# Four edits to a fused decoder-layer kernel: decay-row layout, sample-state engines, weight-sum order, sample-key order

## The chip, the cores and the metric

The kernel runs as one launch on one core of a Trainium2 chip. Five engines work side by side, each on its own instruction list in order: TensorE (PE), VectorE (DVE), ScalarE (ACT), GpSimd (POOL) and SyncE (SP), which here only issues DMAs. The metric is the device time of one execution in microseconds (us); lower is better.

## The reference

One layer of a hybrid decoder is computed for a prompt of 1024 tokens and for 8 single sample tokens, which share all weights. In short:

```python
xn = rmsnorm(x)                                  # prompt and sample tokens
sc_b, sc_c, sc_x, z, xbc, dt, q, gates = split(xn @ w_in)
y_a = (sc_b * conv3(sc_c * sc_x)) @ w_sc_out     # gated convolution
xs, bm, cm = split(silu(conv4(xbc) + bias))      # state-space branch, 32 heads x 64, state 128, 4 groups
# prompt: chunks of 128 tokens; acum = cumsum(dt * a) in the chunk
#   y = (cb * exp(acum_i - acum_j)) @ xdt + exp(acum) * (c @ state);  state = decay * state + b.T @ (...)
# sample: s = s * exp(dt * a) + (dt * x) outer b;   y = s . c         (state_ssm in, s_ssm out)
y_b = group_rmsnorm((y + d * xs) * silu(z)) @ w_ssm_out
y_c = softmax(q . mem_k / 16) @ mem_v @ w_attn_o # prompt: keys from mem; sample: cache_mem_k, cache_mem_v
x = x + (g_a * y_a + g_b * y_b + g_c * y_c) @ w_merge_o
x = x + (silu(xn2 @ w_gate) * (xn2 @ w_up)) @ w_down
y = rmsnorm(x)                                   # outputs: y, memory keys and values, all new states
```

## The kernel before

Matrices are held transposed: 128 features on the partitions, the 1032 tokens (1024 + 8) along the row. Every float32 product is made as three products of rounded halves (high with high, high with low, low with high), so each weight block of 128 x 1024 is loaded by SP, rounded to a high half by ACT (`st_split` and `weights`, lines 220 and 146) and its low half is made by DVE. The pool of weight halves has three slots, and `in_turn` (line 110) fixes the order in which they are written.

The stages follow one another. First come the norm and the dt values (`dt_rows`, line 551, writes the cumulated decays to the scratch tensor `ac_d` and their exponentials to `ea_d`). Then the z and xBC columns are projected two blocks at a time by `strassen` (line 274), which needs seven products instead of eight: the first weight block as it stands (A), then sums of blocks that DVE forms in `sa` (S) and `sb` (T, "third weight sums", `st_sums2`, line 266), then D. While the z pairs run, the memory keys and values are projected too (`kv_block`, line 1100), one half block at each `tick()`. `tick` (line 168) takes the next piece of side work from the list `pend`.

Then comes the state-space stage: for each of 4 groups, 8 chunks of pieces `p1`, `p2`, `p3` (line 906 on) run beside ordinary projections (`gemm`, line 180), three pieces to one projection. `load` (736) fetches a chunk's decay rows into `r`, copied to all 128 partitions, `prep` (743) makes the exponentials on ACT, `first`, `second` and `third` use PE and DVE, and one sample token's state goes through `s_load`, `s_step` and `s_read` (lines 870 to 893). In `s_step` DVE makes an outer product, and POOL multiplies the state by its decay and adds. `s_read` stores the state and reduces it on DVE.

The attention stage runs in the same way beside the output projections (`out_part`, line 1424). Prompt heads go through `a_scores`, and three pieces later `a_probs`. The sample's keys (`s_scores`, line 1250) are multiplied by the query on DVE; query and keys share the two buffers of the tag `kc`. After it `s_out` (1295) loads the sample's values. The feed-forward part uses `strassen` again (line 1632 on), and a down projection ends the layer.

The Tile framework orders the instructions of each engine before the run, by the readiness that its own planned times give and by their place in the program; `tc.issue_after(ins)` adds the rule that what is issued in the block on the engine of `ins` comes after it. On the chip each engine, and SP's list of DMAs, then keeps to that order, however long a wait takes.

## Time and profile before

| what | value |
|---|---|
| time, three runs | 2593.17, 2596.79, 2601.07 us (median 2596.79) |
| the profiled execution: time / span of the instructions | 2593.12 / 2591.4 us |
| TensorE (PE) busy | 2520.2 us, 97% |
| VectorE (DVE) busy | 1463.4 us, 56% |
| ScalarE (ACT) busy | 937.1 us, 36% |
| GpSimd (POOL) busy | 184.6 us, 7% |
| mean granted TensorE clock | 0.989 |

"Busy" adds up the time in which an engine runs at least one instruction. In the lists of waits each row names the waiting engine, its output and line, what it waited for, the sum in us, the count and the longest. Rows of the timeline start with start and duration in us; square brackets hold the idle time of the engine before the row and what ended it. "SPq" is SP issuing a DMA. Groups of instructions are shown by line with their count, busy time, mean duration in ns, and the idle time before them.

### The profile page before, as it was taken

The numbers are of one execution on the slowest core, as the hardware profiler recorded it, in microseconds if no ns is written. First come the engines' busy times: TensorE is split into PE (matmuls) and PEld (weight loads), VectorE is DVE, ScalarE is ACT, GpSimd is POOL, SyncE is SP. The second block draws the span as 40 slices with busy tenths as digits, with TensorE's granted clock in tenths as the row PEclk, the third lists the DMA queues.
The fourth block names the chain that finished last, engine by engine and source line by source line (L and its number), as shares of the span: only waits on it lengthen the run. The fifth ranks groups of instructions, "written<-read, shape, count | busy, mean of one in ns | idle before, by whom it ended". The sixth has DMA issues, their size and how long they took to land.

```text
span 2591.4 us, 42766 instructions
## 1 busy us (share of the span) xinstructions
PE 2520.2 (97%) x18037; PEld 2453.2 (95%) x18037; DVE 1463.4 (56%) x2049; ACT 937.1 (36%) x1436; POOL 184.6 (7%) x203
## 2 busy tenths in 40 slices
PE   7999999999999999999999999999999999999998
PEld 6899999989998999999999998999999999999998
DVE  5744586866667555555566633444685445453316
ACT  6643454553332334254352322222443333341202
POOL 0000000013213213123000000000000000000000
PEclk9999999999999999999999999999999999999999
DMA  5244333376646656666387757854442222265211
GB/s 191 94 139 155 118 112 107 123 193 154 163 150 135 173 173 169 182 183 160 115 300 240 271 177 252 291 199 135 136 155 85 74 88 71 77 218 159 66 41 66
DMA packets 394654, 394.59 MB, mean 152 GB/s; under 512 B 15782, under 2 KB 339990, under 8 KB 394455
## 3 DMA queue, kind: packets, MB, share of 16 engines
q1 hardware_dynamic: 375310, 338.90, 43.9%
q10 hardware_dynamic: 19153, 52.96, 5.3%
q8 instruction: 142, 2.33, 0.4%
q14 instruction: 49, 0.40, 0.0%
HBM read 283.57 MB, written 108.45 MB: 151 GB/s over the span
## 4 chain that ended last, share of the span: by engine, by line
PE 68%; DMA 5%; DVE 4%; ACT 1%; issue 1%; POOL 0%; SPq 0%; DVEq 0%; ACTq 0%; POOLq 0%
PE po L192 11%; PE ps_g L192 9%; PE pd L192 8%; PE ps_scc L192 4%; PE pm L1539 4%; PE ps_q L192 4%; PE ps_scx L192 3%; PE ps_scb L192 3%; DMA kc<-in_cache_mem_k_dram 2%; PE py L801 1%; PE pss L819 1%; PE po L793 1%; DMA r<-ac_d 1%; PE u20m L236 1%; PE g20m L236 1%
## 5 line engine op out<-in xcount | busy, mean ns | idle before, releaser
L1681 DVE TENSOR_TENSOR x<-pd,x 128x1032 f32<-128x1032 f32 x24 | 29.6, 1231 | 130.1 <-PE pd L192 130.1
L746 ACT ACTIVATE r<-r,acum 128x128 f32<-128x128 f32 x256 | 78.9, 391 | 36.2 <-DMA r<-ac_d 35.0
L1428 DVE TENSOR_TENSOR gt<-po,gt 128x1032 f32<-128x1032 f32 x24 | 29.5, 1229 | 74.7 <-PE po L192 68.0
L780 POOL TENSOR_TENSOR xdd<-xdt,decst 128x512 f32<-128x512 f32 x32 | 46.6, 1455 | 266.2 <-DVE xdt L776 266.2
L602 DVE SCALAR_TENSOR_TENSOR ax<-u,prm,ax 128x1024 f32<-128x1024 f32 x44 | 56.4, 1281 | 0.2
L886 POOL TENSOR_TENSOR st<-st,xb 128x512 f32<-128x512 f32 x32 | 44.8, 1401 | 36.2 <-DVE xb L880 34.0
L773 ACT COPY bT<-bp 128x128 f32<-128x128 f32 x32 | 8.4, 263 | 105.4 <-DVE cbm L771 105.4
L774 DVE TENSOR_TENSOR r<-r,cbm 128x1024 f32<-128x1024 f32 x32 | 39.1, 1221 | 9.6 <-ACT r L747 8.9
L810 DVE SCALAR_TENSOR_TENSOR x<-x,dpar,yt 128x128 f32<-128x128 f32 x128 | 37.4, 352 | 10.1 <-ACT yt L808 9.2
L832 POOL TENSOR_TENSOR s<-s,cdec 128x512 f32<-128x512 f32 x28 | 39.1, 1397 | 44.9 <-DVE s L825 36.8
L825 DVE TENSOR_TENSOR s<-pss,s 128x512 f32<-128x512 f32 x28 | 19.2, 687 | 36.7 <-PE pss L819 36.7
L819 PE MATMUL pss<-xdd,bT 128*128 128x512 f32 x64 | 33.8, 610 | 5.9 <-ACT bT L773 5.8
L883 POOL TENSOR_TENSOR st<-st,es 128x512 f32<-128x512 f32 x32 | 36.4, 1138 | 19.2 <-DMA st<-in_state_ssm_dram 15.6
L801 PE MATMUL py<-r,xdt 128*64 128x128 f32 x512 | 35.0, 279 | 2.5 <-issue 2.5
L771 DVE TENSOR_TENSOR cbm<-bp,tri 128x128 f32<-128x128 f32 x32 | 9.2, 289 | 46.8 <-PE bp L766 46.8
L747 ACT ACTIVATE r<-r 128x1024 f32<-128x1024 f32 x32 | 33.9, 1059 | 0.7
L797 DVE TENSOR_TENSOR yt<-po,ea 128x512 f32<-128x512 f32 x28 | 19.2, 686 | 25.9 <-PE po L793 25.9
L801 PEld LDWEIGHTS py<-r,xdt 128*64 128x64 f32 x512 | 27.3, 136 | 6.8 <-issue 3.4
L1267 ACT ACTIVATE pr<-psa,mx 128x256 f32<-128x256 f32 x32 | 14.9, 471 | 49.2 <-DVE mx L1265 49.1
L1468 DVE TENSOR_TENSOR gt<-po,gt 128x1032 f32<-128x1032 f32 x8 | 9.9, 1232 | 38.6 <-PE po L192 38.6
L1546 DVE TENSOR_TENSOR x<-pm,xT 128x516 f32<-128x516 f32 x16 | 11.1, 696 | 36.3 <-PE pm L1539 36.2
L1257 DVE TENSOR_TENSOR kc<-kc,qb 128x1024 f32<-128x1024 f32 x16 | 19.6, 1222 | 21.3 <-DMA kc<-in_cache_mem_k_dram 21.3
(7967 smaller groups left out, 8665.5 us busy)
## 6 DMA issues: line engine op xcount, KB each, us to landing
gt<-gt_d SPq DMA_DIRECT2D x32, 516.0 KB
r<-ac_d SPq DMA_DIRECT2D x32, 512.0 KB
gt_d<-g ACTq DMA_DIRECT2D x24, 516.0 KB
mg_d<-gt SPq DMA_DIRECT2D x24, 516.0 KB
mg<-mg_d SPq DMA_DIRECT2D x24, 516.0 KB
xs_d<-ax ACTq DMA_DIRECT2D x22, 516.0 KB
hr<-h_d SPq DMA_DIRECT2D x22, 516.0 KB
zs_d<-z ACTq DMA_DIRECT2D x16, 516.0 KB
```

The source lines that it names most:

```text
L192: PE.matmul(ps[:, n, :CW], wt[:, ks], x[:, n * CW : (n + 1) * CW], start=(k == 0 and i == 0), stop=(k == nk - 1 and i == 2),)
L236: PE.matmul(ps[:, n, :HC], wt[:, ks], x[:, n * HC : (n + 1) * HC], start=(start and kt == 0 and i == 0), stop=(kt == 3 and i == 2), skip_g ...
L602: V.scalar_tensor_tensor(acc[:, :T], u[:, j : j + T], w[j], acc[:, :T], op0=ALU.mult, op1=ALU.add)
L746: S.activation(r[:, h, :], r[:, h, :], AF.Relu, scale=-1.0, bias=acum[:, c, h0 + h : h0 + h + 1])
L774: V.tensor_tensor(r, r, bc(cbm.unsqueeze(1), [P, HPG, P]), op=ALU.mult)
L780: G.tensor_tensor(b3(xdd, HPG), b3(xdt, HPG), bc(decst[:, c, hs].unsqueeze(2), [P, HPG, 64]), op=ALU.mult)
L801: PE.matmul(py[hp : hp + 64, (h // 2) * P : (h // 2 + 1) * P], xdt[:, h * 64 : (h + 1) * 64], r[:, h, :], start=True, stop=True,)
L810: V.scalar_tensor_tensor(xg[t][:, cs], xg[t][:, cs], dpar[:, g * 4 + t : g * 4 + t + 1], yt[:, t, :], op0=ALU.mult, op1=ALU.add,)
L819: PE.matmul(pss, bT, xdd, start=True, stop=True)
L832: ins = G.tensor_tensor(b3(s_new, HPG), b3(state["s"], HPG), bc(cdec[:, c, hs].unsqueeze(2), [P, HPG, 64]), op=ALU.mult,)
L886: G.tensor_tensor(st, st, xb, op=ALU.add)
L1539: PE.matmul(ps[:, n, :HC], wt[:, ks], x[:, half * HT + n * HC : half * HT + (n + 1) * HC], start=(k == 0 and i == 0), stop=(k == KD - 1 an ...
```

## The change

The decay rows are stored so that the rows of one group and chunk lie together: `load` and `load_ea` then read one contiguous run for each partition instead of eight or four, and so does the read of `bc_d`; in return `dt_rows` writes with 20 DMAs instead of 2. The sample state is multiplied by its decay in four ACT instructions and updated by four DVE instructions, one per quarter; POOL no longer takes part, and the store of the state is issued after the load of a later chunk's decay rows. In `strassen` the sums `sb` are formed right after the S sums, and their split stands ahead of the `tick()`. In the attention stage the query has a buffer of its own, the keys are asked for two pieces ahead of their use, the sample work is spread over four pieces per token, `a_probs` stands ahead of `a_scores`, the `issue_after` rules of `both` are gone, the tag `pr` has three buffers instead of four, and the values are asked for ahead of `s_out`.

```diff
--- before.py
+++ after.py
@@ -263,13 +263,16 @@
         V.tensor_add(sa[:, 512:], sa[:, :512], raw1[:, :512])
         return raw1, raw2, sa, st_split(sa, f"{nm}S")
 
-    def st_sums2(raw1, raw2, sa, nm, sums):
+    def st_adds2(raw1, raw2, sa, nm, sums):
         sb = sums(f"{nm}sb")
         V.tensor_add(sb[:, :512], raw1[:, :512], raw2[:, :512])
         V.scalar_tensor_tensor(
             sb[:, 512:], sa[:, 512:], -1.0, raw1[:, 512:], op0=ALU.mult, op1=ALU.subtract
         )
-        return st_split(sb, f"{nm}T")
+        return sb
+
+    def st_sums2(*args):
+        return st_split(st_adds2(*args), f"{args[3]}T")
 
     def strassen(src1, src2, forms, nm, sums, outs, early=None, after_t3=None, ready=None):
 
@@ -299,6 +302,8 @@
             V.tensor_add(sa[:, :512], raw2[:, :512], raw2[:, 512:])
             V.tensor_add(sa[:, 512:], sa[:, :512], raw1[:, :512])
             wS = st_split(sa, f"{nm}S")
+        if ready is None:
+            sb = st_adds2(raw1, raw2, sa, nm, sums)
         prod(pb, wS, 0, "T1", True)
         S.copy(h3(o22), hv(pb))
         prod(pa, wS, 512, "nT2", early is not None)
@@ -310,9 +315,9 @@
             S.copy(o21, o12)
             V.tensor_sub(o22, o22, o12)
             V.tensor_tensor(h3(o12), hv(pa), h3(o12), op=ALU.add)
+        if ready is None:
+            wT = st_split(sb, f"{nm}T")
         tick()
-        if ready is None:
-            wT = st_sums2(raw1, raw2, sa, nm, sums)
         prod(pa, wT, 0, "T3", False)
         if after_t3 is not None:
             after_t3()
@@ -347,9 +352,9 @@
     q_d = dram("q_d", [8, P, TT])
     k_d = dram("k_d", [2, P, D])
     v_d = dram("v_d", [2, P, D])
-    ac_d = dram("ac_d", [HEADS, T])
-    ea_d = dram("ea_d", [HEADS, T])
-    bc_d = dram("bc_d", [GROUPS, 2, NS, P])
+    ac_d = dram("ac_d", [GROUPS, NCK, HPG, P])
+    ea_d = dram("ea_d", [GROUPS, NCK, 2, HPG // 2, P])
+    bc_d = dram("bc_d", [GROUPS, NS, 2, P])
     qs_d = dram("qs_d", [NS, D])
     os_d = dram("os_d", [NS, D])
 
@@ -557,8 +562,12 @@
             c = slice(half * 512, (half + 1) * 512)
             V.tensor_copy(act_[:, c], ps[:HEADS, :])
             S.activation(eat_[:, c], ps[:HEADS, :], AF.Exp)
-        SY.dma_start(ac_d, act_)
-        SY.dma_start(ea_d, eat_)
+        for g in range(GROUPS):
+            hs = slice(g * HPG, (g + 1) * HPG)
+            SY.dma_start(ac_d[g].rearrange("c h p -> h c p"), act_[hs].rearrange("h (c p) -> h c p", p=P))
+            ev_ = eat_[hs].rearrange("h (c p) -> h c p", p=P)
+            for t in range(HPG // 2):
+                SY.dma_start(ea_d[g, :, :, t].rearrange("c w p -> w c p"), ev_[2 * t : 2 * t + 2])
 
     def dt_sample():
 
@@ -725,7 +734,7 @@
         PE.transpose(ps[:NS, P : 2 * P], bcg[1][:, T:TT], ident)
         t = ev_tile(f"bcr{g}", (NS, 2, P))
         S.copy(t, b3(ps[:NS, : 2 * P], 2))
-        SY.dma_start(bc_d[g].rearrange("k b n -> b k n"), t)
+        SY.dma_start(bc_d[g], t)
 
     def ssd_pieces(g, xg, bcg):
         hs = slice(g * HPG, (g + 1) * HPG)
@@ -735,10 +744,9 @@
 
         def load(c):
             nm = f"{g}_{c}"
-            cs = slice(c * P, (c + 1) * P)
             r = sp_tile([P, HPG, P], "r", "r" + nm, 3)
-            SY.dma_start(r, ac_d[hs, cs].unsqueeze(0).to_broadcast([P, HPG, P]))
             live[c] = r
+            return SY.dma_start(r, ac_d[g, c].unsqueeze(0).to_broadcast([P, HPG, P])).ins
 
         def prep(c):
             r = live[c]
@@ -749,11 +757,9 @@
         def load_ea(c):
             ea = None
             if c > 0:
-                cs = slice(c * P, (c + 1) * P)
                 ea = sp_tile([P, 4, P], "ea", f"ea{g}_{c}")
-                eav = ea_d[hs, cs].rearrange("(t two) i -> two t i", two=2)
                 for k in range(2):
-                    SY.dma_start(ea[k * 64 : (k + 1) * 64], eav[k].unsqueeze(0).to_broadcast([64, 4, P]))
+                    SY.dma_start(ea[k * 64 : (k + 1) * 64], ea_d[g, c, k].unsqueeze(0).to_broadcast([64, 4, P]))
             return ea
 
         def first(c):
@@ -871,19 +877,17 @@
             st = sp_tile([P, 4, P], "st", f"st{g}_{b}", 3)
             SY.dma_start(st, s_rows(a["state_ssm"], b))
             bcb = sp_tile([P, 2, P], "bcb", f"bcb{g}_{b}")
-            SY.dma_start(bcb, bc_d[g, :, b, :].unsqueeze(0).to_broadcast([P, 2, P]))
+            SY.dma_start(bcb, bc_d[g, b].unsqueeze(0).to_broadcast([P, 2, P]))
             samp[b] = (st, bcb)
 
         def s_step(b):
             st, bcb = samp[b]
-            xb = sp_tile([P, 4, P], "xb", f"xb{g}_{b}", 1)
-            V.tensor_tensor(
-                xb, bc(bcb[:, 0:1, :], [P, 4, P]), bc(hold["xd"][:, :, b : b + 1], [P, 4, P]), op=ALU.mult
-            )
-            G.tensor_tensor(
-                st, st, bc(es[:, g * 4 : g * 4 + 4, b : b + 1], [P, 4, P]), op=ALU.mult
-            )
-            G.tensor_tensor(st, st, xb, op=ALU.add)
+            for t in range(4):
+                S.activation(st[:, t], st[:, t], AF.Copy, scale=es[:, g * 4 + t, b : b + 1])
+            for t in range(4):
+                V.scalar_tensor_tensor(
+                    st[:, t], bcb[:, 0], hold["xd"][:, t, b : b + 1], st[:, t], op0=ALU.mult, op1=ALU.add
+                )
 
         def s_read(b):
             st, bcb = samp.pop(b)
@@ -907,10 +911,11 @@
                 if c < NCK:
                     first(c)
                 if c + 2 < NCK:
-                    load(c + 2)
+                    state["load"] = load(c + 2)
                 if c > 1:
                     with tc.issue_after(state["xdt"] if c < NCK else state["sum"]):
-                        s_read(c - 2)
+                        with tc.issue_after(state["load"]):
+                            s_read(c - 2)
 
             def p2(c=c):
                 if c > 0:
@@ -1246,20 +1251,24 @@
                 V.tensor_sub(kTl[:, half * 4 : half * 4 + 4, m * P : (m + 1) * P], b3(ps, 4), kh.bitcast(F32))
 
         qbs = {}
+        kcs = {}
+
+        def s_query(b):
+            qbs[b] = at.tile([P, D], F32, tag="qb", bufs=1, name=f"qb{b}")
+            SY.dma_start(qbs[b], qs_d[b : b + 1, :].to_broadcast([P, D]))
+
+        def s_keys(b, m):
+            kcs[b, m] = at.tile([P, D], F32, tag="kc", name=f"kc{b}{m}")
+            SY.dma_start(kcs[b, m], a["cache_mem_k"][0, b, m * P : (m + 1) * P].rearrange("m h d -> m (h d)"))
 
         def s_scores(b, m):
-            if m == 0:
-                qbs[b] = at.tile([P, D], F32, tag="kc", name=f"qb{b}")
-                SY.dma_start(qbs[b], qs_d[b : b + 1, :].to_broadcast([P, D]))
-            qb = qbs[b]
-            kc = at.tile([P, D], F32, tag="kc", name=f"kc{b}{m}")
-            SY.dma_start(kc, a["cache_mem_k"][0, b, m * P : (m + 1) * P].rearrange("m h d -> m (h d)"))
-            V.tensor_mul(kc, kc, qb)
+            kc = kcs.pop((b, m))
+            V.tensor_mul(kc, kc, qbs[b])
             V.tensor_reduce(sc_s[:, m, b, :], b3(kc, AH), axis=AX.X, op=ALU.add)
 
         def softmax(pr, src, n, npart, name):
-            mx = at.tile([P, 2], F32, tag="mx", name="mx" + name)
-            sm = at.tile([P, 2], F32, tag="smx", name="sm" + name)
+            mxs = at.tile([P, 4], F32, tag="mx", name="mx" + name)
+            mx, sm = mxs[:, :2], mxs[:, 2:]
             sv = b3(src, n)
             V.tensor_reduce(mx[:npart, :n], sv, axis=AX.X, op=ALU.max)
             V.tensor_scalar(mx[:npart, :n], mx[:npart, :n], -1.0 / 16.0, None, op0=ALU.mult)
@@ -1281,7 +1290,7 @@
                 PE.transpose(
                     ps[:32, m * P : (m + 1) * P], sc_s[:, m].rearrange("p b h -> p (b h)"), ident
                 )
-            pr = at.tile([P, 2, MEM], F32, tag="pr", bufs=4, name="prs")[:32, :1]
+            pr = at.tile([P, 2, MEM], F32, tag="pr", bufs=3, name="prs")[:32, :1]
             softmax(pr, ps[:32, :MEM], 1, 32, "s")
             s_hold["pr"] = pr
 
@@ -1292,21 +1301,24 @@
                 PE.transpose(ps[:, m * 32 : (m + 1) * 32], pr[:, 0, m * P : (m + 1) * P], ident[:32, :32])
             V.tensor_copy(pTs.rearrange("p m c -> p (m c)"), ps[:, :64])
 
+        def s_values(b):
+            for m in range(2):
+                kcs[b, m] = at.tile([P, D], F32, tag="kc", name=f"vc{b}{m}")
+                SY.dma_start(kcs[b, m], a["cache_mem_v"][0, b, m * P : (m + 1) * P].rearrange("m h d -> m (h d)"))
+
         def s_out(b):
             ps = sm_ps(f"pso{b}")
-            vcs = []
-            for m in range(2):
-                vc = at.tile([P, D], F32, tag="kc", name=f"vc{b}{m}")
-                SY.dma_start(vc, a["cache_mem_v"][0, b, m * P : (m + 1) * P].rearrange("m h d -> m (h d)"))
-                vcs.append(vc)
+            vcs = [kcs.pop((b, m)) for m in range(2)]
             for m in range(2):
                 for h in range(AH):
                     PE.matmul(
                         ps[32 * h : 32 * h + 32, :256], pTs[:, m, :], vcs[m][:, h * 256 : (h + 1) * 256],
                         start=(m == 0), stop=(m == 1),
                     )
-            t = at.tile([P, 256], F32, tag="so", bufs=1, name=f"so{b}")
+            t = at.tile([P, 2, MEM], F32, tag="pr", bufs=3, name=f"so{b}")[:, 0]
             S.copy(t, ps[:, :256])
+            if b + 1 < NS:
+                s_values(b + 1)
             for h in range(AH):
                 row = 32 * h + b * AH + h
                 SY.dma_start(os_d[b : b + 1, h * 256 : (h + 1) * 256], t[row : row + 1, :])
@@ -1343,7 +1355,7 @@
                     PE.matmul(po, qh[:, ls], kh, start=(dk == 0), stop=False)
                     PE.matmul(po, qh[:, ls], kl, start=False, stop=False)
                     PE.matmul(po, ql[:, ls], kh, start=False, stop=(dk == 1))
-            pr = at.tile([P, 2, MEM], F32, tag="pr", bufs=4, name="pr" + nm)
+            pr = at.tile([P, 2, MEM], F32, tag="pr", bufs=3, name="pr" + nm)
             heads[h][2][l2] = pr
             return softmax(pr, ps, 2, P, nm)
 
@@ -1378,35 +1390,28 @@
                 S.copy(ot[:, c], ps)
             S.dma_start(at_d[2 * h + dk, :, :T], ot[:, :T])
 
-        def both(*fs):
-
-            def run():
-                ins = fs[0][0](*fs[0][1:]) if fs else None
-                for f, *args in fs[1:]:
-                    if ins is None:
-                        f(*args)
-                    else:
-                        with tc.issue_after(ins.ins):
-                            f(*args)
-
-            return run
-
-        pieces = [both((kv_in, 0)), both((kv_in, 1), (a_load, 0)), None, None]
-        side = deque([(s_scores, b, m) for b in range(NS) for m in range(2)])
-
-        def aside():
-            return (side.popleft(),) if side else ()
-
+        pieces = [[(kv_in, 0)], [(kv_in, 1), (a_load, 0)], [], []]
         for h in range(AH):
             for l2 in range(LAG + 4):
-                fs = [(a_scores, h, l2)] if l2 < 4 else []
                 late = [(a_probs, h, l2 - LAG)] if l2 >= LAG else []
-                pieces.append(both(*fs, *aside(), *late) if fs else both(*late, *aside()))
+                pieces.append(late + ([(a_scores, h, l2)] if l2 < 4 else []))
             if h + 1 < AH:
-                pieces.append(both((a_load, h + 1)))
-            pieces.append(both((a_out, h, 0)))
-            pieces.append(both((a_out, h, 1)))
-        pieces += [s_softmax, None, s_probs, None]
+                pieces.append([(a_load, h + 1)])
+            pieces.append([(a_out, h, 0)])
+            pieces.append([(a_out, h, 1)])
+        for b in range(NS):
+            at_ = 4 + 4 * b
+            for i, fs in enumerate(
+                ([(s_query, b), (s_keys, b, 0)], [(s_keys, b, 1)], [(s_scores, b, 0)], [(s_scores, b, 1)])
+            ):
+                pieces[at_ + i].extend(fs)
+
+        def run(fs):
+            for f, *args in fs:
+                f(*args)
+
+        pieces = [lambda fs=fs: run(fs) for fs in pieces]
+        pieces += [s_softmax, lambda: s_values(0), s_probs, None]
         for b in range(NS):
             pieces += [lambda b=b: s_out(b), None]
         pend.extend(pieces)
```

## The prediction

> **What bounds the kernel.** The first look goes to the page: how busy is each engine over the whole span?
>
> ```profile
> span 2591.4 us, 42766 instructions
> PE 2520.2 (97%) x18037; PEld 2453.2 (95%) x18037; DVE 1463.4 (56%) x2049; ACT 937.1 (36%) x1436; POOL 184.6 (7%) x203
> ```
>
> PE works for 2520.2 of 2591.4 us. The change takes no matrix product away, so all that it can win lies in the 71.2 us in which PE stands. The second look, the table of busy times by stretch, says where these are.
>
> ```profile
> core 0: us, PE busy (x) PEld busy (x) DVE busy (x) ACT busy (x) POOL busy (x), PEclk, DMA share, GB/s
> 100.00:300.00 200.00, 187.19 (x1516) 183.83 (x1515) 92.25 (x129) 85.73 (x127) 0.17 (x3) 0.97 0.43 136
> 540.00:1000.00 460.00, 447.88 (x2994) 429.05 (x2995) 289.80 (x414) 162.70 (x307) 113.32 (x99) 0.99 0.62 160
> 1000.00:1300.00 300.00, 299.30 (x2000) 287.65 (x1999) 164.35 (x240) 127.69 (x190) 62.05 (x48) 1.00 0.58 164
> 1300.00:1470.00 170.00, 159.59 (x1002) 154.99 (x1001) 113.77 (x158) 62.85 (x117) 0.00 (x0) 0.97 0.81 275
> 1860.00:1960.00 100.00, 93.59 (x745) 92.19 (x744) 76.35 (x115) 44.45 (x67) 0.00 (x0) 0.97 0.39 125
> ```
>
> PE stands for 12.8 us in the z pairs (100 to 300), 12.1 us in the first part of the state-space stage (540 to 1000), 0.7 us in the rest of it, 10.4 us beside the attention (1300 to 1470) and 6.4 us where the feed-forward part begins. These are 42.4 us; the others lie at the start and the end, which the change does not touch. The third look, the list of PE's waits, gives each one a cause.
>
> ```profile
> PE pss L819 <- ACT bT L773: 5.8, 1, 5.8
> PE psp L1357 <- DVE b05l L163: 3.7, 1, 3.7
> PE Z4m L236 <- ACT Z4Th L223: 2.5, 1, 2.5
> PE py L801 <- issue: 2.5, 1, 2.5
> PE xp L769 <- DVE yt L806: 2.5, 1, 2.5
> PE Z12m L236 <- ACT Z12Th L223: 2.5, 1, 2.5
> PE Z8m L236 <- ACT Z8Th L223: 2.5, 1, 2.5
> PE psp L1357 <- ACT pr L1267: 2.1, 1, 2.1
> PE g2m L236 <- DVE g2o L312: 1.8, 1, 1.8
> PE u2m L236 <- DVE u2o L312: 0.9, 1, 0.9
> ```
>
> The change aims at exactly these places. Their sum, 5.8 + 3.7 + 3 x 2.5 + 2 x 2.5 + 2.1 + 1.8 + 0.9 = 26.8 us, is about the most that it can bring.
>
> **Third weight sums.** The timeline around Z4, DVE and ACT rows together:
>
> ```profile
> 150.69 0.69 DVE L308 TENSOR_TENSOR z<-Z4m,z 128x516 f32<-128x516 f32 x1 [5.67 <-PE Z4m L236]
> 151.30 0.68 DVE L268 TENSOR_TENSOR Z4sb<-Z4r,Z4r 128x512 f32<-128x512 f32 x1
> 153.08 0.71 ACT L1120 COPY kv<-ps_kv 128x256 f32<-128x256 f32 x2 [3.59 <-PE ps_kv L1115]
> 154.81 1.04 ACT L223 CAST Z4Th<-Z4sb 128x1024 fp32r<-128x1024 f32 x1 [1.03 <-issue]
> 155.89 1.23 DVE L224 TENSOR_TENSOR Z4Tl<-Z4sb,Z4Th 128x1024 fp32r<-128x1024 f32 x1 [3.31 <-ACT Z4Th L223]
> ```
>
> The sums stand behind the addition of line 308, which waits for PE's fourth product, and the rounding Z4Th stands behind the copies of the memory keys, which come out of the `tick()`. DVE had been idle for 5.67 us before; the sums need nothing but the loaded blocks and `sa`. Moved up they fill that idle time, and the rounding goes ahead of the tick. Nothing is added: the same two sums, one cast and one subtraction. The three waits of 2.5 us (Z4, Z8, Z12) should go, -7.5. The same edit removes g2's 1.8 and u2's 0.9 us, where the sums stand behind lines 311 and 312: -2.7. The pair g0 gets its sums ready-made and keeps its wait. What could come late next is the second memory half block, which now queues behind Z4Th for one of three slots: it may use the slot of S, whose product ends before PE needs T. I charge nothing; the bound is all 7.5 back.
>
> **Decay rows and the order of the store.** Rows of the waits (the first two), the chain of waits (the next two) and the timeline around 830:
>
> ```profile
> ACT r L746 <- DMA r<-ac_d: 35.0, 7, 17.1
> SPq L890 <- POOL st L886: 173.1, 29, 12.2
> ...
> 831.67 10.90 DMA r<-ac_d
> 1357.20 3.44 DMA kc<-in_cache_mem_k_dram
> ...
> 828.50 2.16 POOL L886 TENSOR_TENSOR st<-st,xb 128x512 f32<-128x512 f32 x1
> 830.68 0.38 SPq L890 DMA_DIRECT2D out_s_ssm_dram<-st  x1
> 831.67 0.66 SPq L740 DMA_DIRECT2D r<-ac_d  x1
> 842.65 0.98 ACT L746 ACTIVATE r<-r,acum 128x128 f32<-128x128 f32 x3 [17.07 <-DMA r<-ac_d]
> ```
>
> SP stood until POOL had finished a state (830.66), issued its store, and only then `r`; `r` took 10.90 us to land, and ACT stood 17.07 us with `bT` queued behind the exponentials. That is PE's longest wait, 5.8 us. The keys `kc` have the same 512 KB in rows of 4 KB, where `r` comes in pieces of 512 B, and landed in 3.44 us. The new `r` has rows of 4 KB too, so I estimate 3.5 to 6 us, and it no longer queues behind the store. The waits of `py` (at the first chunk, whose `r` is also asked for at once) and of `xp` (behind another late `r`) go the same way. Together 5.8 + 2.5 + 2.5 = 10.8 us; bounds 0 and -10.8. I take -9, since the first chunk of the stage can hide only part of its load. From 1000 on PE stands for 0.7 us: nothing to win.
>
> **Sample states.** Unit costs, from the groups of instructions, and last a row of POOL's waits:
>
> ```profile
> L746 ACT ACTIVATE r<-r,acum 128x128 f32<-128x128 f32 x256 | 78.9, 391 | 36.2 <-DMA r<-ac_d 35.0 <-ACT bT L773 1.2
> L810 DVE SCALAR_TENSOR_TENSOR x<-x,dpar,yt 128x128 f32<-128x128 f32 x128 | 37.4, 352 | 10.1 <-ACT yt L808 9.2
> L880 DVE TENSOR_TENSOR xb<-bcb,xds 128x512 f32<-128x512 f32 x32 | 22.0, 689 | 0.0
> L883 POOL TENSOR_TENSOR st<-st,es 128x512 f32<-128x512 f32 x32 | 36.4, 1138 | 19.2 <-DMA st<-in_state_ssm_dram 15.6 <-DVE xb L880 3.6
> ...
> POOL st L883 <- DMA st<-in_state_ssm_dram: 15.6, 3, 7.0
> ```
>
> In each of 32 steps ACT gains four instructions of 128 x 128, 4 x 0.391 = 1.56 us (50 us in all); DVE loses one of 0.689 and gains four of 0.352, +0.72 us (23 us); POOL loses its two. ACT is busy for 162.70 of 460 us and DVE for 289.80 there, so both have room: I charge 0. If the cover were gone, 23 us of DVE or 50 us of ACT would be the worst end. What changes is who waits: POOL used to wait for the landing of the state (15.6 us in three places), and nothing but POOL's own work was behind it. Now ACT waits there in order, with `bT`, the exponentials and the roundings of weights behind it. This is the main danger, taken up below.
>
> [...]
>
> **Sample keys.** The row of DVE's waits and the two waits of `psp` above belong together:
>
> ```profile
> DVE kc L1257 <- DMA kc<-in_cache_mem_k_dram: 21.3, 10, 6.7
> ```
>
> The query holds one of two `kc` buffers through both halves, so the second half's keys can only be asked for when the first half is done, and DVE stands for 21.3 us with the softmax behind it. With a buffer for the query and requests two pieces ahead, most of that goes. PE's part is 2.1 + 3.7; but at the 3.7 PE's wait ends with b05l, one of eight split activations for the next projection, which remain. Bounds 0 and -5.8; I take -3. Reordering and the third `pr` buffer in place of a fourth move no work; a probability tile must now be transposed before the next softmax writes, and `a_probs` stands first for that: 0.
>
> **Writing the decay rows.**
>
> ```profile
> 104.00 0.32 SPq L560 DMA_DIRECT2D ac_d<-acT  x1
> 106.04 0.68 DVE L576 COPY exs<-dtT 8x1024 f32<-8x1024 f32 x1 [0.86 <-DMA ac_d<-acT]
> 107.84 0.32 SPq L561 DMA_DIRECT2D ea_d<-eaT  x1
> ```
>
> Twenty issues instead of two are 18 x 0.32 = 5.8 us more of SP. The weights behind them are loaded well ahead, but `exs` needs the buffer of `acT`, and its DVE copy already waits for that DMA. With four writes it comes 3 x 0.32 = 1 us later; if SP has the writes interleaved with those of `ea_d`, which start at 107.84, some 8 us later. PE's dt transposes follow. Bounds 0 and +8; I take +2, close to the former, since the first rows are ready about 4 us earlier.
>
> **The sum.** -7.5 - 2.7 - 9 + 0 - 3 + 2 = -20.2 us. The profiled execution took 2593.12 us (its span 2591.4), 3.7 below the median of the runs, 2596.79. So 2573 for such an execution and 2577 for the median.
>
> **The rivals.**
>
> *Slower: ACT waits for the states.* The state's load is issued behind DVE's read of `bcb` and behind an earlier store, and its landing time is not what the order was planned with: POOL met it late in three places, up to 7.0 us. If the four decays are placed early in ACT's order, ACT stands at each late state. The `r` that ACT waited for at 842 cost PE 5.8 us for a wait of 17.07, about a third. From 0.65 us of PE per step on, 32 steps eat the 20 us. At a wait of 4 us per step and a third of it on PE, 32 x 1.3 = 43 us are lost: 2577 + 43 = 2620. Against it: ACT idles for 65% of that stage, and the state is loaded two chunks ahead. Chance 0.16.
>
> *No change: the stalls move.* The memory half blocks take the place of T in the fixed order of the weight halves, giving back the 7.5, and the attention's two waits turn out to belong to the split activations, giving back 3; with half of the 9 us of `r` lost too, 15 of 20.2 are gone: 2592. For it: all these waits are short and on engines that are lightly loaded, and another input may be late just behind. Against: DVE stood idle for 5.67 us with T's inputs at hand. Chance 0.15.
>
> *More than forecast:* all of 26.8 us go, and the writing of the rows costs nothing: 2570. It lies inside the forecast.
>
> **How the numbers follow.** 0.3% of this kernel is 7.8 us, about the spread of the three runs, and what a measurement can tell. The forecast has 0.69, its own range 2566 (all waits, and an execution like the fastest) to 2588. For the whole I reach into both rivals: 2562 to 2604. Faster by over 0.3%: 0.69; within: 0.15; slower: 0.16.
>
> **What would show it.** In the new profile PE's waits for Z4Th, Z8Th, Z12Th and behind lines 311 and 312 are gone; `r` lands within about 6 us and ACT's wait of 35.0 us falls below 12; POOL keeps only the products for `xdd` and the decayed chunk state (and small copies); DVE's wait of 21.3 us for `kc` falls to a few us; PE's busy time stays near 2520. The forecast is wrong if ACT shows a long wait for the state's DMA with PE behind it, if PE waits for `ps_ex` near 110, or if new waits at the memory blocks replace those at T.

## The result and the profile after

The changed kernel takes 2574.99 us (median of 4 runs, 2574.20 to 2576.87) against 2594.98 us before (median of 4 beside them): 0.9920 of the time, 95% interval 0.9902 to 0.9938. In a second comparison it was 2574.11 to 2594.92 us, 0.9922 [0.9911, 0.9934]. So 20 us are gone, about what was forecast (2577, -20.2). The total is right; several of the terms behind it are not, as will be seen.

First the page of the changed kernel, span and PE:

```profile
span 2572.8 us, 42933 instructions
PE 2513.5 (98%) x18037; PEld 2448.3 (95%) x18037; DVE 1484.8 (58%) x2145; ACT 977.7 (38%) x1565; POOL 94.8 (4%) x139
```

The span is 18.6 us shorter (2591.4 to 2572.8). PE stands for 59.3 us instead of 71.2, which is 11.9; the other 6.7 are busy time (2520.2 to 2513.5) with the same 18,037 products. The same products took fewer microseconds, and the mean granted clock of the two executions is 0.989 and 0.991: 0.2% of 2520 us is about 5 us. This comes back at the sums.

The table of busy times by stretch (same stages as before; the last one moved with the feed-forward part):

```profile
100.00:300.00 200.00, 189.28 (x1549) 186.81 (x1548) 94.09 (x131) 88.21 (x131) 0.17 (x3) 0.97 0.44 136
540.00:1000.00 460.00, 460.00 (x3103) 441.48 (x3103) 304.74 (x486) 194.13 (x404) 60.93 (x64) 1.00 0.54 165
1000.00:1300.00 300.00, 298.94 (x1989) 287.80 (x1989) 177.32 (x269) 137.64 (x224) 24.07 (x19) 1.00 0.54 171
1300.00:1470.00 170.00, 160.72 (x991) 155.49 (x990) 110.84 (x158) 63.66 (x120) 0.00 (x0) 0.96 0.79 266
1843.00:1943.00 100.00, 93.02 (x753) 91.62 (x752) 78.01 (x116) 44.60 (x68) 0.00 (x0) 0.98 0.38 123
```

Read the first number behind the length against the length: PE's idle time goes from 12.8 to 10.7 us in the z pairs, from 12.1 to 0 in the first part of the state-space stage, from 0.7 to 1.1 in its rest, from 10.4 to 9.3 beside the attention, from 6.4 to 7.0 in the feed-forward part. Nearly all the idle time that went, went in one place. The list of PE's waits gives the causes of what is left there:

```profile
PE ps_mt L1094 <- DVE mem L1089: 5.4, 1, 5.4
PE psa L1355 <- DVE b07l L163: 2.6, 1, 2.6
PE psa L1355 <- ACT pr L1276: 1.8, 1, 1.8
PE g2m L236 <- DVE g2o L317: 1.6, 1, 1.6
PE u2m L236 <- DVE u2o L317: 1.6, 1, 1.6
```

The waits of 2.5 us for Z4Th, Z8Th and Z12Th are gone, and so are those of `pss`, `py` and `xp` in the state-space stage. Those behind the feed-forward sums are not (1.8 and 0.9 before, 1.6 and 1.6 now). One is new: 5.4 us at the transposes of the memory, `ps_mt`. Last, rows from the waits of ACT, DVE and SP:

```profile
ACT st L886 <- DMA st<-in_state_ssm_dram: 67.6, 20, 6.6
ACT r L754 <- DMA r<-ac_d: 10.0, 2, 5.6
...
DVE kc L1266 <- DMA qb<-qs_d: 20.2, 5, 10.5
...
SPq L894 <- DVE st L888: 56.7, 14, 7.8
```

ACT's wait for the decay rows fell from 35.0 to 10.0 us, as forecast. DVE's wait in the sample attention did not fall: its 21.3 us for the keys became 20.2 us for the query. SP stands 56.7 instead of 173.1 us for the finished state. And ACT stands for 67.6 us at the states' loads: the slower rival named just this, yet PE has no idle time behind it here.

### The profile page after: what moved, and what is told of

Read it like the earlier page. It is cut to its first block, busy times and chain, and to the rows that moved or that the text cites. A ratio compares the mean times of both kernels' runs of the same rounds, so it can differ in the third digit from the quotient of the medians.

```text
span 2572.8 us, 42933 instructions
## 1 busy us (share of the span) xinstructions
PE 2513.5 (98%) x18037; PEld 2448.3 (95%) x18037; DVE 1484.8 (58%) x2145; ACT 977.7 (38%) x1565; POOL 94.8 (4%) x139
## 4 chain that ended last, share of the span: by engine, by line
PE 88%; DMA 4%; DVE 4%; ACT 2%; issue 1%; SPq 0%; ACTq 0%; DVEq 0%
PE po L192 11%; PE ps_g L192 9%; PE pd L192 8%; PE pm L1544 4%; PE ps_scc L192 4%; PE ps_scx L192 4%; PE ps_scb L192 4%; PE ps_q L192 4%; PE py L807 1%; PE pss L825 1%; PE po L799 1%; PE Z2m L236 1%; PE ps_z L192 1%; PE X17m L236 1%; PE Z4m L236 1%
## 5 line engine op out<-in xcount | busy, mean ns | idle before, releaser
L886 ACT ACTIVATE st<-st,es 128x128 f32<-128x128 f32 x128 | 41.9, 391 | 83.5 <-DMA st<-in_state_ssm_dram 67.6
L888 DVE SCALAR_TENSOR_TENSOR st<-bcb,xds,st 128x128 f32<-128x128 f32 x128 | 58.6, 516 | 0.0
L838 POOL TENSOR_TENSOR s<-s,cdec 128x512 f32<-128x512 f32 x28 | 30.2, 1079 | 55.0 <-DVE s L831 46.6
L1266 DVE TENSOR_TENSOR kc<-kc,qb 128x1024 f32<-128x1024 f32 x16 | 19.5, 1220 | 21.8 <-DMA qb<-qs_d 20.2
L807 PEld LDWEIGHTS py<-r,xdt 128*64 128x64 f32 x512 | 27.3, 136 | 4.2 <-issue 0.9
L1437 DVE TENSOR_TENSOR gt<-gt,mg 128x1032 f32<-128x1032 f32 x16 | 19.7, 1230 | 18.7 <-DMA mg<-mg_d 18.6
```

What stands on the lines that cost most here:

```text
L807: PE.matmul(py[hp : hp + 64, (h // 2) * P : (h // 2 + 1) * P], xdt[:, h * 64 : (h + 1) * 64], r[:, h, :], start=True, stop=True,)
L886: S.activation(st[:, t], st[:, t], AF.Copy, scale=es[:, g * 4 + t, b : b + 1])
L888: V.scalar_tensor_tensor(st[:, t], bcb[:, 0], hold["xd"][:, t, b : b + 1], st[:, t], op0=ALU.mult, op1=ALU.add)
```

## The experiments

The theory after the result: the layout removes `r`'s late landings and so the 12 us of the state-space stage; the state edit is free; the sums give 7.5 to 10 us. The rivals: the gain comes from the order of the store, not from the rows; the state edit costs time which the other parts pay for, or it is itself what frees the loads. Each part was tried alone on the kernel before, or undone in the changed one.

| kernel | median us | before | ratio, 95% | difference |
|---|---|---|---|---|
| only_sums | 2581.99 | 2595.24 | 0.9952 [0.9940, 0.9965] | -13.3 |
| only_layout | 2592.85 | 2595.24 | 0.9988 [0.9979, 0.9998] | -2.4 |
| only_state | 2625.98 | 2595.24 | 1.0123 [1.0108, 1.0138] | +30.7 |
| only_order | 2595.06 | 2595.24 | 1.0002 [0.9992, 1.0011] | -0.2 |
| only_keys | 2588.73 | 2593.63 | 0.9980 [0.9971, 0.9988] | -4.9 |
| no_layout | 2620.97 | 2593.63 | 1.0107 [1.0094, 1.0120] | +27.3 |
| no_state | 2570.70 | 2593.63 | 0.9913 [0.9900, 0.9926] | -22.9 |
| rows_first | 2570.93 | 2593.63 | 0.9912 [0.9898, 0.9926] | -22.7 |
| rows_first_pool | 2569.92 | 2594.92 | 0.9901 [0.9887, 0.9915] | -25.0 |
| after_again (the changed kernel) | 2574.11 | 2594.92 | 0.9922 [0.9911, 0.9934] | -20.8 |
| before_state_dve | 2587.87 | 2594.92 | 0.9976 [0.9965, 0.9986] | -7.1 |
| pe_stalls | 2571.63, one run | | | |

The five parts alone add up to -13.3 - 2.4 + 30.7 - 0.2 - 4.9 = +9.9 us; together they give -20. So some 30 us are an interaction, and it lies between the layout and the state edit.

### The sums alone

```diff
+        if ready is None:
+            sb = st_adds2(raw1, raw2, sa, nm, sums)
         prod(pb, wS, 0, "T1", True)
...
+        if ready is None:
+            wT = st_split(sb, f"{nm}T")
         tick()
-        if ready is None:
-            wT = st_sums2(raw1, raw2, sa, nm, sums)
```

> The kernel before with the third weight sums made early, and nothing else. By the prediction -10.2 us (the waits at Z4, Z8, Z12 and behind lines 311 and 312 go). By what the trace of the changed kernel shows (g2 and u2 still wait 1.6 us each) only the z part: -7.5 us, and somewhat more if a short wait also costs PE clock: the trace before has half clock for 3.4 us after the waits at Z4 and Z12. Rival (the stalls move): within 2 us of no change.

-13.3 us, where the prediction had -10.2. The stretch of the z pairs in this kernel, and one of its two waits in the feed-forward part:

```profile
100.00:300.00 200.00, 194.10 (x1600) 191.48 (x1599) 96.48 (x134) 88.59 (x131) 0.17 (x3) 0.99 0.45 143
```

```profile
PE g2m L236 <- DVE g2o L317: 2.2, 1, 2.2
```

Idle time falls from 12.8 to 5.9 us, the three waits for T. The feed-forward term gave nothing: the wait of g2 stands where it was (1.8 us before, 2.2 here; u2 has 0.9 and 0.7), so the sums were not what PE waited for there. The row itself says what was: `g2o` is the addition that empties the tile `pa` (line 312 of the kernel before), which the next product, T3, overwrites. That leaves about 7 us of idle time against a gain of 13. The rest is the clock. The table of busy times of the kernel before, around its wait for Z4Th; the third number from the right is the granted clock:

```profile
153.40:155.90 2.50, 0.00 (x0) 0.00 (x0) 0.01 (x1) 1.47 (x4) 0.00 (x0) 0.97 0.79 215
155.90:159.20 3.30, 3.29 (x15) 3.29 (x16) 2.95 (x3) 1.43 (x2) 0.00 (x0) 0.51 0.45 155
...
217.80:221.20 3.40, 3.36 (x28) 3.37 (x29) 2.96 (x3) 1.45 (x2) 0.00 (x0) 1.00 0.49 166
...
278.30:281.60 3.30, 3.27 (x16) 3.27 (x17) 2.96 (x3) 1.44 (x2) 0.00 (x0) 0.55 0.37 128
```

and the same place with only the sums moved:

```profile
155.90:159.20 3.30, 3.30 (x30) 3.30 (x29) 1.39 (x2) 0.89 (x2) 0.00 (x0) 1.00 1.00 268
```

Behind the wait of 2.5 us PE is "busy" for 3.3 us but does 15 products where it otherwise does 30: the clock is at 0.51. The last two rows are the stretches behind the waits for Z8Th (no slow clock) and Z12Th (0.55). So two of the three waits cost about 2.5 + 3.3 x 0.5 = 4.2 us and one 2.5, which makes 10.8 of the 13.3 us (interval 9 to 16). Standing for 2.5 us was followed by some 3.3 us at about half clock twice out of three times here.

### The layout alone, and the order of the store alone

```diff
-        SY.dma_start(ac_d, act_)
-        SY.dma_start(ea_d, eat_)
+        for g in range(GROUPS):
+            hs = slice(g * HPG, (g + 1) * HPG)
+            SY.dma_start(ac_d[g].rearrange("c h p -> h c p"), act_[hs].rearrange("h (c p) -> h c p", p=P))
+            ev_ = eat_[hs].rearrange("h (c p) -> h c p", p=P)
+            for t in range(HPG // 2):
+                SY.dma_start(ea_d[g, :, :, t].rearrange("c w p -> w c p"), ev_[2 * t : 2 * t + 2])
...
-            SY.dma_start(r, ac_d[hs, cs].unsqueeze(0).to_broadcast([P, HPG, P]))
+            SY.dma_start(r, ac_d[g, c].unsqueeze(0).to_broadcast([P, HPG, P]))
```

> The kernel before with the decay rows (and the sample's B and C rows) contiguous, and nothing else. By the prediction most of the 10.8 us of the state-space stage go, less up to 8 us for the twenty writes: -2 to -9 us. Rival: the wait at 842 us came from the store that stood in front of the load, so the layout alone leaves a wait of ACT on the decay rows of more than 5 us there, and the time stays within 3 us or rises by up to 5 us through the writes (a wait of PE near 143 us as in the changed kernel).

```diff
-                    load(c + 2)
+                    state["load"] = load(c + 2)
...
-                        s_read(c - 2)
+                        with tc.issue_after(state["load"]):
+                            s_read(c - 2)
```

> The kernel before with the store of a state issued after the load of the later decay rows, and nothing else. If the store in front of the load is the cause of the late rows, the waits of 5.8 and 2.5 us (bT, xp) go: -6 to -10 us. If the 512 B pieces are the cause, under 3 us either way.

The order alone changes nothing (-0.2 us): PE waits 6.4 us for `bT` (5.8 before) and ACT 35.3 us for `r` (35.0 before). But it does not test what it was made for. Each store now stands behind one more load of `r`; at the place of the long wait SP still has a store right ahead of `r`, and stands for POOL before it (6.5 us). The timeline of only_order, SP and ACT rows:

```profile
833.26 0.38 SPq L890 DMA_DIRECT2D out_s_ssm_dram<-st  x1
834.29 0.61 SPq L741 DMA_DIRECT2D r<-ac_d  x1
845.83 0.98 ACT L746 ACTIVATE r<-r,acum 128x128 f32<-128x128 f32 x3 [17.66 <-DMA r<-ac_d]
```

What the rows of 4 KB change is the transfer. In the chain of waits of only_layout the same `r`, which landed in 10.90 us before, has:

```profile
837.62 7.16 DMA r<-ac_d
```

SP still stands for POOL ahead of it (181.8 us in all), so it is asked for no sooner; ACT waits 13.3 us there instead of 17.07, and PE 2.1 us for `bT` instead of 5.8. The rival of only_layout had named such a wait of over 5 us as its sign, so both the transfer and the place behind the store have a part. The layout alone gives only -2.4 us. Its stretches:

```profile
100.00:300.00 200.00, 178.54 (x1425) 176.11 (x1424) 85.82 (x119) 81.23 (x121) 0.00 (x0) 0.93 0.39 124
540.00:1000.00 460.00, 455.00 (x3075) 436.86 (x3074) 297.46 (x427) 168.65 (x314) 114.53 (x102) 1.00 0.56 169
```

It wins 7.1 us of idle time in the state-space stage (12.1 to 5.0) and loses 8.7 in the z pairs (12.8 to 21.5), with the clock down to 0.93 there. Counted in products, 1425 instead of 1516 at some 7.6 per us, that loss is worth about 12 us (an estimate from these rows), and the gain of 3075 to 2994 products in the other stretch about as much. With the sums moved too, as in the changed kernel, the loss of idle time is 10.7 - 5.9 = 4.8. The loss comes with the twenty small writes; in the timeline of the changed kernel SP issues them so:

```profile
103.94 0.99 SPq L567 DMA_DIRECT2D ac_d<-acT  x3
107.75 3.71 SPq L570 DMA_DIRECT2D ea_d<-eaT  x12
111.51 0.28 SPq L567 DMA_DIRECT2D ac_d<-acT  x1
```

The fourth write of `ac_d`, on which the buffer for `exs` waits, stands behind twelve writes of `ea_d` which must wait for the exponentials. The wait of `ps_mt`, 5.5 us in this kernel, comes with this part: no kernel with the old layout shows it. The rows give the chain: the first copy `exs` starts at 106.04 us before, at 113.90 here and at 125.87 in the changed kernel, and the memory's norm on ACT, which comes ahead of `ps_mt`, starts behind PE's transposes of these copies, at 113.91, 123.60 and 137.88. In the changed kernel:

```profile
137.88 1.06 ACT L1084 ACTIVATE memh<-mem 128x1024 fp32r<-128x1024 f32 x1 [6.24 <-PE ps_ex L590]
```

### The state edit alone

```diff
-            V.tensor_tensor(
-                xb, bc(bcb[:, 0:1, :], [P, 4, P]), bc(hold["xd"][:, :, b : b + 1], [P, 4, P]), op=ALU.mult
-            )
-            G.tensor_tensor(
-                st, st, bc(es[:, g * 4 : g * 4 + 4, b : b + 1], [P, 4, P]), op=ALU.mult
-            )
-            G.tensor_tensor(st, st, xb, op=ALU.add)
+            for t in range(4):
+                S.activation(st[:, t], st[:, t], AF.Copy, scale=es[:, g * 4 + t, b : b + 1])
+            for t in range(4):
+                V.scalar_tensor_tensor(
+                    st[:, t], bcb[:, 0], hold["xd"][:, t, b : b + 1], st[:, t], op0=ALU.mult, op1=ALU.add
+                )
```

> The kernel before with the sample states on ScalarE and VectorE, and nothing else; the store still stands ahead of the load. By the prediction 0. Rival 1: POOL's two instructions were what SP waited for, so the wait of 5.8 us for bT goes with them: -6 to -10 us. Rival 2: ACT waits for the states' DMA with PE behind it: +5 us or more.

+30.7 us: the slower rival came true. Stretches, then waits of ACT and PE in this kernel:

```profile
540.00:1000.00 460.00, 440.97 (x2914) 421.76 (x2915) 290.60 (x457) 179.64 (x374) 54.72 (x59) 0.98 0.61 157
1000.00:1300.00 300.00, 287.42 (x1903) 273.18 (x1903) 164.94 (x271) 135.66 (x237) 29.43 (x24) 0.99 0.55 154
```

```profile
ACT st L880 <- DMA st<-in_state_ssm_dram: 103.1, 18, 10.3
...
PE bp L765 <- DVE yt L797: 11.0, 5, 3.1
```

One such place in the timeline, ACT, DVE and PE rows:

```profile
605.93 1.28 ACT L880 ACTIVATE st<-st,es 128x128 f32<-128x128 f32 x4 [9.17 <-DMA st<-in_state_ssm_dram]
607.12 1.03 ACT L152 CAST wscc2h<-wscc2r 128x1024 fp32r<-128x1024 f32 x1
608.18 1.23 DVE L153 TENSOR_TENSOR wscc2l<-wscc2r,wscc2h 128x1024 fp32r<-128x1024 f32 x1 [7.14 <-ACT wscc2h L152]
609.32 0.68 DVE L797 TENSOR_TENSOR yt<-po,ea 128x512 f32<-128x512 f32 x1
610.06 0.48 PE L765 MATMUL bp<-ident,bc 128*128 128x128 f32 x1 [2.59 <-DVE yt L797]
```

ACT stands 9.17 us for a state; behind it in order is the rounding of a weight block; DVE stands 7.14 us for that; its next instruction is the one PE waits for, 2.59 us. None of these depend on the state. ACT is busy for 179.64 of 460 us, so it is not the work that costs but its place in the order. The rival's sum took a wait of 4 us per step and a third of it on PE; measured are 103.1 / 32 = 3.2 us per step, and 30.7 us in all are 0.30 of 103.1. Its opposite argument, that the state is loaded two chunks ahead, is what failed: the first decay starts 6.9 us behind the issue of its load here, on average over the 32 steps (loads and decays paired in order), where POOL's in the kernel before starts 17 us or more behind it.

### The layout undone, and the state edit undone, in the changed kernel

no_layout puts the old shapes, the two whole writes and the old loads of `r`, `ea` and `bcb` back and keeps all else, the order of the store too. no_state puts `xb` and the two POOL instructions back.

> The changed kernel with the decay rows (and B and C rows) laid out as before. The state edit alone cost 31 us, with ACT waiting 103 us for the states' DMA. If the contiguous rows are what takes that cost away (fewer pieces in front of the states in SP's list), this kernel loses it again: 2590 to 2615 us, ACT waiting over 90 us for the states. If the store's place is what takes it away, it stays at 2570 to 2580 us. By my own sum it would be 2575 + 9 - 2 = 2582.

> The changed kernel with the sample states on POOL as before. If the state edit is worth nothing once the rows are contiguous (my sum), 2573 to 2578 us. If it gives what the layout alone does not (PE still stood 2.1 us for bT there, SP 182 us for POOL), 2580 to 2590 us. If it still costs, below 2570 us.

no_layout is 27.3 us slower than before, 47 to 48 slower than the changed kernel, though it lacks one part only. Its stretch and its waits for the state:

```profile
540.00:1000.00 460.00, 439.47 (x2908) 419.80 (x2907) 285.43 (x449) 177.84 (x373) 55.00 (x59) 0.98 0.58 152
```

```profile
ACT st L885 <- DMA st<-in_state_ssm_dram: 143.0, 24, 10.5
...
SPq L877 <- DMA out_s_ssm_dram<-st: 78.2, 21, 8.0
```

SP, about to load a state, waits 78.2 us for stores of earlier states to land; in the changed kernel that row has:

```profile
SPq L878 <- DMA out_s_ssm_dram<-st: 24.1, 10, 6.4
```

With the long rows ACT's waits for the states halve (143.0 to 67.6 us) and get short enough (6.6 at most) to be covered: idle time in the stretch is 20.5 us with the old rows and 0 with the new. Of ACT's idle time right ahead of its decays, whatever ended it, 153 us with the old rows and 83 with the new, 50 and 12 us lie before the load is issued at all, where SP asks for the state late; behind the issue there are 103 and 72 us. That the layout does it is shown, though not which of its three tables (`r`, `ea`, `bcb`); that it does so because the short rows held up the other transfers is the reading of these rows. SP's waits for stores cost nothing by themselves: only_order has 85.4 us of them. And the parts alone would add up to +12.3 us for no_layout (30.7 - 13.3 - 0.2 - 4.9), where +27.3 were measured: without the long rows the state edit also gets 15 us dearer beside the other parts. Which of them does that was not separated. no_state at -22.9 (without the state edit the parts alone add up to -20.8) shows that the state edit, even so, brings nothing; the changed kernel stood at -20.0 and -20.8 in other comparisons, so it may cost 2 to 3 us, which is at the edge of what can be told.

### The decay on DVE instead of ACT

Before with the state's decay as one DVE instruction and the four DVE updates, nothing on ACT or POOL:

```diff
             V.tensor_tensor(
-                xb, bc(bcb[:, 0:1, :], [P, 4, P]), bc(hold["xd"][:, :, b : b + 1], [P, 4, P]), op=ALU.mult
-            )
-            G.tensor_tensor(
                 st, st, bc(es[:, g * 4 : g * 4 + 4, b : b + 1], [P, 4, P]), op=ALU.mult
             )
-            G.tensor_tensor(st, st, xb, op=ALU.add)
+            for t in range(4):
+                V.scalar_tensor_tensor(
+                    st[:, t], bcb[:, 0], hold["xd"][:, t, b : b + 1], st[:, t], op0=ALU.mult, op1=ALU.add
+                )
```

> The kernel before with the sample states on VectorE alone: one decay instruction of 128 x 512, then the four updates; no ACT, no POOL. If the 31 us of the state edit come from ACT waiting in order for the states' DMA, they go: within 5 us of the kernel before. If they come from VectorE's four updates standing ahead of the drain of po and py (PE waited 11.0 us for yt), they stay: +20 us or more.

-7.1 us, where the same decay on ACT took +30.7 on the same kernel. The stretch:

```profile
540.00:1000.00 460.00, 454.85 (x3066) 436.06 (x3065) 315.28 (x502) 163.04 (x307) 64.55 (x63) 1.00 0.61 164
```

Idle time 5.2 us instead of 12.1, with the old rows. DVE reaches 315 of 460 us and still hides it. That it is faster than before, by more than the 5 us expected, the rows put down to SP. Its wait for the finished state, and PE's for `bT`, in this kernel:

```profile
SPq L889 <- DVE st L883: 98.9, 27, 10.8
PE pss L819 <- ACT bT L773: 1.4, 1, 1.4
```

Before they were 173.1 and 5.8 us, and the waits of `py` and `xp` fall from 2.5 to 1.1 us each: 7.2 us together. This is rival 1 of the state edit (POOL was what SP waited for, and -6 to -10 us go with it), which ACT's waits had hidden there (SP's wait falls to 109.2 us in only_state too).

Engine and place changed together, though. DVE's decay starts at least 28 us behind the issue of its load, and no row of DVE's waits names a state, where ACT's in only_state starts 6.9 us behind it on average. So the case shows what a decay on ACT at its early place costs, not what a late one would. The decay on DVE in the changed kernel was not run. The two versions lie 38 us apart (+30.7 and -7.1); what the runs show behind this is that ACT stands in order at a load that has not landed (103.1 us in only_state), with more urgent work behind it.

### The keys alone

```diff
-            if m == 0:
-                qbs[b] = at.tile([P, D], F32, tag="kc", name=f"qb{b}")
+            qbs[b] = at.tile([P, D], F32, tag="qb", bufs=1, name=f"qb{b}")
...
+        for b in range(NS):
+            at_ = 4 + 4 * b
```

> The kernel before with the attention edit alone. By the prediction -3 us (bounds 0 and -5.8). By the trace of the changed kernel, where PE stands 9.3 us between 1300 and 1470 as against 10.4 before and new waits of 1.8 and 2.6 us stand at psa: within 2 us of no change.

-4.9 us (predicted -3; the second expectation, within 2 us of no change, was wrong). The stretch beside the attention, and a row of DVE's waits there:

```profile
1300.00:1470.00 170.00, 159.67 (x1017) 154.14 (x1017) 114.12 (x160) 65.65 (x122) 0.00 (x0) 0.99 0.83 279
```

```profile
DVE kc L1261 <- DMA qb<-qs_d: 9.6, 4, 4.4
```

DVE now waits for the query (9.6 us). PE's idle time is 10.3 us, as before (10.4), but 1017 products were done in the stretch instead of 1002, at a clock of 0.99 instead of 0.97: 2% of 160 us is about 3 us. So the gain is in how the waits are cut up rather than in their sum; which change of order did that was not separated.

### The writes put in another order, and the best version

rows_first issues the four writes of `ac_d` ahead of the sixteen of `ea_d`; rows_first_pool does that and leaves the sample states on POOL.

```diff
             SY.dma_start(ac_d[g].rearrange("c h p -> h c p"), act_[hs].rearrange("h (c p) -> h c p", p=P))
-            ev_ = eat_[hs].rearrange("h (c p) -> h c p", p=P)
+        for g in range(GROUPS):
+            ev_ = eat_[g * HPG : (g + 1) * HPG].rearrange("h (c p) -> h c p", p=P)
             for t in range(HPG // 2):
```

> The changed kernel with the four writes of ac_d ahead of all sixteen of ea_d. If the wait of PE at 143 us (5.4 us, then half clock) comes from the copies exs being planned behind the last write of ac_d, it goes: -5 to -9 us, 2566 to 2570 us. If the wait belongs to the memory's own norm, no change.

> The changed kernel with the four writes of ac_d first and with the sample states back on POOL. Each of the two alone came out about 4 us below the changed kernel in another call. If both are real and independent: 2566 to 2568 us, 7 to 9 below the changed kernel. If one was noise: about 4 below.

> The changed kernel once more, beside the two below on one chip: 2573 to 2577 us, ratio 0.992.

rows_first takes 2570.93 us, and its z pairs lose a little less (the stretch, and the row of PE's waits):

```profile
100.00:300.00 200.00, 190.92 (x1575) 188.31 (x1574) 95.20 (x133) 89.72 (x132) 0.17 (x3) 0.98 0.44 137
```

```profile
PE ps_mt L1095 <- DVE mem L1090: 5.0, 1, 5.0
```

9.1 us of idle time instead of 10.7. The wait of `ps_mt` stays (5.0 us), so the place of these four writes is not its cause alone. Here `exs` starts at 109.22 us and PE's transposes of it are done at 118.7, but ACT takes up the memory's norm only at 132.61, behind the work of the z blocks that stands ahead of it in ACT's order; why the order has it there is open. rows_first_pool has the lowest median, 2569.92 us, 0.9901 [0.9887, 0.9915] of before, and 4.2 us below after_again on the same chip, whose interval (0.9911 to 0.9934) it just touches. It beats the kernel before clearly and the changed kernel by a margin that is hardly more than the measurement. From rows_first (0.9912) and no_state (0.9913) it can't be told apart, and by its own expectation 4 us means that one of the two gains was noise.

### Waits made on purpose

To price a wait of PE by itself, copies of a finished product into an unused tile were added on ACT ahead of the product T4 of four pairs (6, 8, 10 and 14 copies of some 0.59 us each); nothing is left out.

```diff
+        for _ in range({"g8": 6, "u10": 8, "g14": 10, "u16": 14}.get(nm, 0)):
+            S.copy(stj[0], hv(pa))
         prod(pa, wD, 0, "T4", False)
```

> The changed kernel with ScalarE copying the third product 6, 8, 10 and 14 times into an unused tile, ahead of the seventh product of four feed-forward pairs (g8, u10, g14, u16), where PE ran without a pause at full clock. Waits of PE of about 0.8, 2, 3 and 5.5 us. If a wait alone lowers the granted clock, half clock for 3.4 us or more follows the longer ones and not the shortest, and each long wait costs more than its length. Rival: the clock dips belong to their stages, and none follows here; the time rises by the waits' sum, about 11 us.

One time, 2571.63 us, beside 2574.11 for the kernel without the copies. No wait came about: the order of the work put the next pair's products in the place, and no wait of a microsecond stands at any of the four. The run says nothing about the price of a wait. The traces hold an answer in another way, by counting the waits that came about by themselves; it stands at the end.

## Why the prediction was right, and where it was not

**The bound** was right: PE's idle time set what could be won, and 11.9 of the 18.6 us are idle time. That PE's busy time would stay near 2520 was wrong by 6.7 us: the argument took a wait at its length, and half clock stood behind some of the waits too (0.51 and 0.55 behind two of the three for T).

**Third weight sums, -7.5 and -2.7.** The first part was right in mechanism and too small: the three waits went and gave about 10.8 with the clock. The second failed: "the same edit removes g2's 1.8 and u2's 0.9 us" did not happen (1.6 and 1.6 us after). It misread its row, which ends with `g2o` of line 312 and not with T: PE waited for that addition itself, not for the sums behind it. The sum, -10.2 against -13.3 measured, is near for a partly wrong reason. The bound "all 7.5 back" through the memory half blocks did not come.

**Decay rows and store order, -9.** The waits of 5.8, 2.5 and 2.5 us went, and in the changed kernel the estimate of 3.5 to 6 us for the landing holds where ACT waits for it; in only_layout it took 7.16 us. In the changed kernel's timeline at the first chunk, where the load is waited for at once:

```profile
542.11 0.80 SPq L749 DMA_DIRECT2D r<-ac_d  x2
547.74 1.57 ACT L754 ACTIVATE r<-r,acum 128x128 f32<-128x128 f32 x5 [4.45 <-DMA r<-ac_d]
```

It is issued from 542.11 and read at 547.74, 5.6 us. The step "it no longer queues behind the store" has support, but not from only_order, which left the store in front at the long wait: before_state_dve, where SP stands 98.9 instead of 173.1 us for the states, has 1.4 us of the 5.8 left with the old rows, and the layout alone 2.1. Alone the layout won 7.1 us of idle time in this stage, near the -9, but it was not asked what else the long rows would free; that was the larger effect.

**Sample states, 0.** Here lies the real error, which the total hides. The step "both have room: I charge 0" holds only with the new layout; alone the edit costs 30.7 us, and the rival's 43 us was a fair size for it. The "main danger" was named rightly, but its chance of 0.16 was given without joining it to the other term (the states' loads and `r` are issued by the same SP), and it leaned on "the state is loaded two chunks ahead", where ACT's decays came 6.9 us behind the load's issue. DVE's update was mis-sized too. In the changed kernel's groups, and in its timeline:

```profile
L888 DVE SCALAR_TENSOR_TENSOR st<-bcb,xds,st 128x128 f32<-128x128 f32 x128 | 58.6, 516 | 0.0
```

```profile
783.48 1.92 DVE L888 SCALAR_TENSOR_TENSOR st<-bcb,xds,st 128x128 f32<-128x128 f32 x4
783.64 1.08 POOL L838 TENSOR_TENSOR s<-s,cdec 128x512 f32<-128x512 f32 x1 [2.92 <-DVE s L831]
...
788.10 1.14 DVE L816 SCALAR_TENSOR_TENSOR x<-x,dpar,yt 128x128 f32<-128x128 f32 x4
```

A mean of 516 ns, not the 352 taken from line 810, because 28 of the 128 updates took about 1.14 us; it was hidden.

**Sample keys, -3.** -4.9 measured alone, inside the bounds of 0 and -5.8, but not by the way foretold: the wait moved from the keys to the query and hardly fell.

**Writing the decay rows, +2.** Too low. In only_layout the z pairs have 8.7 us more idle time, just above the upper bound of +8, and with the clock the loss is nearer 12; beside the sums the idle time is 4.8 us more. The prediction named the interleaving ("some 8 us later"), which is what SP did, and chose the other end. The sign it gave, a wait of PE for `ps_ex` near 110, was the right place (2.3 us in only_layout); the long wait itself came later, at `ps_mt`.

**The rival of no change** was right in kind in two places: the wait for the keys became one for the query, and the wait of 5.4 us at `ps_mt` is new, though it comes from the writes and not from T taking a slot.

**The sum** of the terms alone as measured is +9.9, the whole -20. Adding up terms took them as independent; the state edit's price depends on the layout by 28 us or more (30.7 alone, 2.9 in the changed kernel). That the total came out right is in part luck: the 0 for the states held only because the two parts were made together, and the sums and keys, too small by 3.1 and 1.9 us, made up for the writes.

## What to carry to other kernels

An instruction moved to an engine that is two thirds idle can still cost tens of microseconds (30.7 us here, on ACT, which had been busy for 162.70 of 460 us), when it waits there for a load and urgent work stands behind it in order: look at what the new engine has queued and how soon behind the load's issue it gets there, not at its busy share. When a change has several parts, ask of each whether its cover comes from another part; here the waits for the states' loads were only covered because other tables' rows had become longer (no_layout +27.3 us against before, the changed kernel -20). And price a wait of the tensor engine with what follows it: the granted clock in the stretch behind it belongs to its cost (0.51 for 3.3 us behind the wait for Z4Th).
